# A decoder trunk on one core: the causal mask in VectorE's maximum, the forget gates' sums at the first HGRN2 step, the opening's norm in other tiles

## The chip, the core and the metric

The kernel runs on one core of a Trainium2 chip. Its engines work side by side, each through its own queue in strict order: TensorE (PE in the profile; PEld are its weight loads), VectorE (DVE), ScalarE (ACT), GpSimd (POOL) and SyncE (SP), which mostly issues DMAs. Semaphores tie them together. The metric is the device time of one execution in microseconds (us); less is better. The number given for a kernel is the median of its runs; the profile is of one more execution.

## The reference

Two layers, each a half-step SwiGLU, a mixer of three kinds of heads, and another half-step SwiGLU, with an RMSNorm ahead of each; 512 tokens, width 1024, all in float32. What the change touches is the opening (the first RMSNorm), the forget gates' running sum, and the masked softmax of the attention:

```python
for l in range(DEPTH):                                            # 2
    x = x + 0.5 * swiglu(rms_norm(x, ffn1_norm[l]), ffn1_w_in[l], ffn1_w_out[l])
    h = rms_norm(x, mix_norm[l]) @ w_mix_in[l]
    ...
    y = concat([short_conv_mixer(...), hgrn2_mixer(...), fox_mixer(...)])
    x = x + y @ w_mix_out[l]
    x = x + 0.5 * swiglu(rms_norm(x, ffn2_norm[l]), ffn2_w_in[l], ffn2_w_out[l])

def fox_mixer(q, k, v, f_logit, f_bias, q_gain, k_gain):         # 8 heads of 64
    ...
    log_f = log_sigmoid(f_logit + f_bias)
    cum = cumsum(log_f, axis=1).transpose(0, 2, 1)
    def block(i):                                                # 128 queries
        s = einsum('bhqd,bhkd->bhqk', qb, kh) + (cb[..., :, None] - cum[..., None, :])
        s = where(qpos[:, None] >= kpos[None, :], s, MASK_VALUE)
        p = softmax(s, axis=-1)
        return einsum('bhqk,bhkd->bhqd', p, vh)
```

## The kernel before, in words

Activations lie with features on the 128 partitions and the 512 tokens along a row. A float32 operand is split into a high half (a cast to fp32r) and a low half, the rest; a product takes three matmuls, high by high, high by low and low by high (`mm3`, lines 318, 324, 325). Weights come from HBM in granules: SP issues the DMAs into a tile `st` (line 290, two buffers), ACT casts the high half into a tile `hl` (line 307, three buffers), VectorE subtracts for the low half (line 308), and PE multiplies. The big matrices of the SwiGLU go through a scheme of halved products that adds and subtracts quarters first (lines 759 to 907).

What runs first on each engine is set by a tile scheduler from the order of the source and from priorities. Buffers come from pools: a tile asked for by a tag gets the next buffer of that tag, and its first writer waits until the readers of the tile that had it are done. Where `follow` is called, the order on an engine is fixed by hand; the DMAs of the opening on SP are one such chain.

**The opening** (`cover`, `open_stream`) runs in the first layer's first SwiGLU. It loads x, transposes it, scales it, and multiplies it with the first weight columns (lines 1657, 1666, 1667, 1710) while the squares for the norm are summed (`sqa`). `parted_norm` (line 418) splits the sum of squares into two tiles `sh`, two matmuls with a matrix of 1/1024 give the mean on all partitions (line 430), and `end_norm` makes `inv` of it. `lower_bounds` (line 944) then loads a few logits of HGRN2 into a tile `lb` of tag g1 (line 956). The two `sh` tiles have the tag g1 as well, with two buffers. `cover` goes on with the next weight columns, whose granules come from line 290.

**The mixer.** Ahead of HGRN2 its projections are made; the last of them also gives the attention's forget logits `zf`. `hgrn` is a generator of steps: after each the program takes a number of steps from `projections()`, the attention's q, k and v products, which keep PE busy. Its steps use the PSUM banks `pt` for transposes (line 1253) and for the output (`T`, line 1409). After it, `fox_decay` (line 1425) takes zf through log-sigmoid (lines 1429 to 1436), forms the running sum with eight matmuls by an upper triangle `utri` (line 1440, in a `pt` bank), and scales it into `negc` on ACT (line 1445) and VectorE (line 1446). `fox_prep` transposes q and k for each head (line 1495) and takes negc in as extra rows of the products.

**The attention** (`fox_attend`) runs in two halves of four heads. An item is a head and one of four query blocks i, over (i + 1) × 128 keys. `scores` puts two matmuls (lines 1521, 1522) and a third, the mask (line 1523: the identity by a tile of −1e30 above the diagonal, bf16), into a bank of PSUM; VectorE takes the negated maximum (line 1526); ACT takes the exponential with it as bias and sums the row (line 1528, printed as L270 since a helper issues it; from PSUM into a tile P of three buffers); VectorE inverts the sum (line 1529) and scales P (line 1533; ACT for i = 3). The scores run three items ahead (LOOK = 3). Item n is then transposed (line 1584), split (lines 1586, 1587) and multiplied with V (line 1543). Between them the program places the short convolution's and the output projection's matmuls as filler, each with its weight granules.

## Time and profile before

| what | us |
| --- | --- |
| runs | 1835.08, 1830.63, 1832.18 |
| median | 1832.18 |
| profiled execution | 1827.76 |
| its span, first to last instruction | 1826.0 |
| granted TensorE clock over it | 0.998 of full speed |

In a timeline row the first figure is the start in us from the span's beginning, the second the duration of what the row holds, then the engine, the line and the operation, output and inputs, their shape, and how many instructions were put together. In square brackets stands how long the engine had been idle before it and the instruction that ended the wait. In a row of a group (`x64: 230/231/236`) the durations are in ns: least, median, most. In a row of windows each engine's busy time follows its stretch and length, in the order PE, PEld, DVE, ACT, POOL, then the clock and the DMA engines' share. The two layers' attention runs from 484 to 588 and from 1383 to 1487 us.

### The profile page before, as it was taken

To read this page: it belongs to the slowest core of one execution; us is meant where nothing else is said; L and a number is where in the kernel's file an instruction comes from. 1 tells how busy PE (TensorE), PEld (TensorE's weight loads), DVE (VectorE), ACT (ScalarE), POOL (GpSimd) and SP (SyncE) were. 2 spreads that over 40 slices of the span, in tenths; PEclk is the share of its full clock that TensorE was granted. 3 is DMA by queue.
4 is the path that set the end of the run, shared out by engine and by line. 5 is a ranking of instruction groups with operands and counts; after the bars stand their busy time and mean duration, and the time that the engine had idled before them with its cause. 6 is when DMAs were issued, how large, how long until landed. Compare 5 with 4: busy or idle time off the path is not lost.

```text
span 1826.0 us, 34831 instructions
## 1 busy us (share of the span) xinstructions
PE 1809.0 (99%) x14345; PEld 1684.3 (92%) x14345; DVE 1466.3 (80%) x2017; ACT 989.9 (54%) x1402; POOL 169.5 (9%) x168
## 2 busy tenths in 40 slices
PE   8999999999999999999999999999999999999999
PEld 6899999899878899999889999998997788999997
DVE  8788888676797988879678887866858878888883
ACT  5455555454675565555445555555547665555551
POOL 0011020100000001112001111201000000020210
PEclk9999999999999999999999999999999999999999
DMA  5849684233322767868265787813333228677762
GB/s 147 233 109 199 171 174 113 70 88 83 87 71 92 216 141 163 191 168 174 81 193 137 162 191 194 165 64 82 83 82 82 76 93 231 162 152 195 153 137 92
DMA packets 243935, 250.94 MB, mean 137 GB/s; under 512 B 18457, under 2 KB 229153, under 8 KB 243777
## 3 DMA queue, kind: packets, MB, share of 16 engines
q1 hardware_dynamic: 189872, 182.38, 32.8%
q0 software_dynamic: 53600, 66.09, 22.7%
q8 instruction: 112, 1.84, 0.4%
q14 instruction: 47, 0.38, 0.1%
q10 hardware_dynamic: 304, 0.27, 0.0%
HBM read 223.98 MB, written 2.10 MB: 124 GB/s over the span
## 4 chain that ended last, share of the span: by engine, by line
PE 92%; DVE 3%; ACT 3%; DMA 1%; issue 1%; SPq 0%; ACTq 0%; DVEq 0%
PE mm L318 13%; PE mm L325 13%; PE mm L324 13%; PE sc L325 6%; PE sc L324 6%; PE sc L318 6%; PE pt L318 6%; PE pt L324 6%; PE pt L325 6%; PE po L318 3%; PE po L324 3%; PE po L325 3%; PE po L1543 1%; PE sc L1710 1%; PE pt L1710 1%
## 5 line engine op out<-in xcount | busy, mean ns | idle before, releaser
L786 ACT CAST hl<-w 128x1024 fp32r<-128x1024 f32 x322 | 337.5, 1051 | 317.9 <-PE mm L325 76.8
L788 DVE TENSOR_TENSOR hl<-w,hl 128x1024 fp32r<-128x1024 f32 x322 | 392.7, 1222 | 85.8 <-ACT hl L786 85.6
L307 ACT CAST hl<-st 128x512 fp32r<-128x512 f32 (+2 forms) x188 | 142.2, 756 | 190.3 <-PE po L325 67.8
L308 DVE TENSOR_TENSOR hl<-st,hl 128x512 fp32r<-128x512 f32 (+2 forms) x188 | 161.6, 860 | 100.3 <-ACT hl L307 98.6
L318 PE MATMUL mm<-xc,hl 128*128 128x256 f32 (+1 forms) x732 | 201.7, 276 | 0.5 <-ACT g L897 0.5
L325 PE MATMUL mm<-xc,hl 128*128 128x256 f32 x728 | 201.6, 277 | 0.0
L324 PE MATMUL mm<-xc,hl 128*128 128x256 f32 x728 | 201.5, 277 | 0.0
L325 PE MATMUL sc<-xc,hl 128*128 128x256 f32 x528 | 146.0, 277 | 0.0
L318 PE MATMUL sc<-xc,hl 128*128 128x256 f32 (+1 forms) x530 | 146.0, 276 | 0.0
L324 PE MATMUL sc<-xc,hl 128*128 128x256 f32 x528 | 145.9, 276 | 0.0
L318 PEld LDWEIGHTS mm<-xc,hl 128*128 128x128 f32 x732 | 137.3, 188 | 0.8 <-ACT g L897 0.7
L324 PEld LDWEIGHTS mm<-xc,hl 128*128 128x128 f32 x728 | 137.0, 188 | 0.0
L325 PEld LDWEIGHTS mm<-xc,hl 128*128 128x128 f32 x728 | 136.7, 188 | 0.1
L318 PE MATMUL pt<-xc,hl 128*128 128x256 f32 (+1 forms) x484 | 132.9, 276 | 0.0
L324 PE MATMUL pt<-xc,hl 128*128 128x256 f32 x480 | 132.7, 277 | 0.0
L325 PE MATMUL pt<-xc,hl 128*128 128x256 f32 x480 | 132.5, 276 | 0.0
L318 PE MATMUL mm<-x,hl 128*128 128x512 f32 x272 | 108.5, 399 | 6.0 <-ACT hl L307 5.6
L324 PE MATMUL mm<-x,hl 128*128 128x512 f32 x272 | 107.5, 395 | 0.0
L325 PE MATMUL mm<-x,hl 128*128 128x512 f32 x272 | 107.1, 394 | 0.0
L318 PEld LDWEIGHTS sc<-xc,hl 128*128 128x128 f32 x530 | 99.5, 188 | 0.2
L325 PEld LDWEIGHTS sc<-xc,hl 128*128 128x128 f32 x528 | 99.1, 188 | 0.1
L324 PEld LDWEIGHTS sc<-xc,hl 128*128 128x128 f32 x528 | 99.1, 188 | 0.0
(510 smaller groups left out, 5618.2 us busy)
## 6 DMA issues: line engine op xcount, KB each, us to landing
w<-in_ffn_w_in_dram SPq DMA_DIRECT2D x140, 512.0 KB, 5.2
w<-in_ffn_w_out_dram SPq DMA_DIRECT2D x64, 512.0 KB, 4.5
w<-in_ffn_w_out_dram POOLq DMA_DIRECT2D x56, 512.0 KB, 8.6
st<-in_w_mix_in_dram SPq DMA_DIRECT2D x88, 256.0 KB, 2.7
st<-in_ffn_w_in_dram SPq DMA_DIRECT2D x70, 256.0 KB, 3.3
w<-in_ffn_w_in_dram POOLq DMA_DIRECT2D x35, 512.0 KB, 8.5
w<-S POOLq DMA_DIRECT2D x35, 512.0 KB, 4.8
st<-in_ffn_w_out_dram SPq DMA_DIRECT2D x24, 512.0 KB, 4.6
```

Of the source, the lines that this page charges most:

```text
L307: a = nc.scalar.copy(hi, src[:, c : c + w])
L308: b = nc.vector.tensor_sub(lo, src[:, c : c + w], hi)
L318: i = nc.tensor.matmul(acc[:, c], ah, bh[:, c], start=first and c.start == 0, stop=False, skip_group_check=True,)
L324: nc.tensor.matmul(acc, ah, bl, start=False, stop=False, skip_group_check=True)
L325: i = nc.tensor.matmul(acc, al, bh, start=False, stop=last, skip_group_check=True)
L786: A(nc.scalar.copy(hi, src))
L788: return lambda: V(nc.vector.tensor_sub(lo, src, hi))
L1543: nc.tensor.matmul(self.ob[:, t0 + u * P : t0 + 2 * P], V[:, j, h % 4].rearrange("p a d -> p (a d)"), part[:, j, u:, :].rearrange("p i t - ...
L1710: E(nc.tensor.matmul(acc, wh[j][l][:, cols], (self.xh, self.xl)[r][k + j], start=k + j == 0 and which == 0, stop=k + j == KD - 1 and which ...
```

## The change

Three places change, and the tile `identb` (the identity in bf16) goes with the mask's matmul. In the opening the two `sh` tiles get the tags r0 and r1; the later callers keep theirs. `fox_decay` is called when the first step of `hgrn` has been issued. In the attention the third matmul goes; an instruction of VectorE adds a mask tile to the scores, negates the sum, writes it to P and takes the minimum, which is the bias as before; the exponential reads P in place with the scale −1. The mask tile (`zmask`, bf16, 384 zeros and the 128 of `maskb`) is made on GpSimd in each layer.

```diff
-        self.identb = c.tile([P, P], BF16, tag="identb", name="identb")
-        nc.vector.tensor_copy(self.identb, self.ident)
...
-    def parted_norm(self, pool, tag, bufs, keep=False):
-        nc = self.nc
-        hi, lo = (pool.tile([P, T], F32R, tag=tag, name=self.n("sh"), bufs=bufs) for _ in range(2))
+    def parted_norm(self, pool, tags, bufs, keep=False):
+        nc = self.nc
+        hi, lo = (pool.tile([P, T], F32R, tag=tag, name=self.n("sh"), bufs=bufs) for tag in tags)
...
             def norm():
                 self.end_norm(
                     self.bank("pt" if self.ntog % 2 == 0 else "po"), fp,
-                    self.parted_norm(fp, "g1", 2),
+                    self.parted_norm(fp, ("r0", "r1"), 1),
                 )
...
                 dense = projections()
-                for n in self.hgrn(l, hp, z, q, v, sg, og):
+                for part, n in enumerate(self.hgrn(l, hp, z, q, v, sg, og)):
+                    if part == 0:
+                        self.fox_decay(mp, zf)
                     for _ in range(n):
                         next(dense, None)
-                self.fox_decay(mp, zf)
...
+                self.zmask = ap_.tile([P, T], BF16, tag="zm", name=self.n("zm"))
+                nc.gpsimd.memset(self.zmask[:, : T - P], 0.0)
+                nc.gpsimd.tensor_copy(self.zmask[:, T - P :], self.maskb)
...
-            nc.tensor.matmul(sb[:, :n], QB[:, c], KB[:, :n], start=False, stop=False)
-            nc.tensor.matmul(sb[:, c], self.identb, self.maskb, start=False, stop=True)
+            nc.tensor.matmul(sb[:, :n], QB[:, c], KB[:, :n], start=False, stop=True)
             s1 = lambda tag: pool.tile([P, 1], F32, tag=tag, name=self.n(tag), bufs=3)
             nm, rs = s1("nm"), s1("rs")
-            nc.vector.tensor_reduce(nm, sb[:, :n], axis=AX.X, op=ALU.max, negate=True)
             pb = tl("P", 3)
-            self.act(pb[:, :n], sb[:, :n], AF.Exp, bias=nm, accum_out=rs)
+            nc.vector.tensor_tensor_reduce(
+                pb[:, :n], sb[:, :n], self.zmask[:, T - n :], -1.0, 3e38, ALU.add, ALU.min, nm
+            )
+            self.act(pb[:, :n], pb[:, :n], AF.Exp, bias=nm, scale=-1.0, accum_out=rs)
```

The lines move by a few: 290, 307, 318, 421, 430, 956 of before are 288, 305, 316, 419, 428, 954 now, 1253 and 1440 are 1255 and 1442, and 1526, 1529, 1533, 1584 are 1528, 1532, 1536, 1587.

In the opening, on SP, the last DMAs of `open_stream` (st_296), then `lb` and the next granules, with what each waits for; before:

```order
L1657 DMA st_296<-in_ffn_w_in_dram 128x2x256 [waits DMAHW2_49,DVE_49]
L1657 DMA st_296<-in_ffn_w_in_dram 128x2x256 [waits DMAHW3_49]
L956 DMA lb_457<-in_hgrn_lb_logits_dram 128x4x1 [waits DMAHW4_49,DVE_49,PE_49]
L290 DMA st_504<-in_ffn_w_in_dram 128x2x256 [waits DMAHW7_49,DMAHW6_49,DMAHW5_49]
L290 DMA st_504<-in_ffn_w_in_dram 128x2x256
```

and now:

```order
L1660 DMA st_296<-in_ffn_w_in_dram 128x2x256 [waits DMAHW2_49,DVE_49]
L1660 DMA st_296<-in_ffn_w_in_dram 128x2x256 [waits DMAHW3_49]
L954 DMA lb_455<-in_hgrn_lb_logits_dram 128x4x1 [waits DMAHW4_49]
L288 DMA st_502<-in_ffn_w_in_dram 128x2x256 [waits DMAHW6_49,DMAHW7_49,DMAHW5_49,DVE_49]
L288 DMA st_502<-in_ffn_w_in_dram 128x2x256
```

`lb` no longer waits for PE or VectorE, and the first granule waits for VectorE itself. On ACT, in the same place, the cast of this granule (hl_507, now hl_505) stood behind `sh` and the norm's activations:

```order
L1666 COPY hl_299<-st_296 128x512
L391 ACTIVATE x_48_305<-po_271,gain_88 128x512
L1666 COPY hl_299<-st_296 128x512
L407 ACTIVATE sq_323<-mm_266 128x512
L407 ACTIVATE sq_327<-po_271 128x512
L421 COPY sh_411<-sqa_158 128x512
L270 ACTIVATE nr_417<-po_410,epsc 128x512
L270 ACTIVATE nr_417<-nr_417 128x512
L270 ACTIVATE nt_418<-nr_417 128x512
L307 COPY hl_507<-st_504 128x1024
```

and now:

```order
L1669 COPY hl_299<-st_296 128x512
L305 COPY hl_505<-st_502 128x1024
L389 ACTIVATE x_48_305<-po_271,gain_88 128x512
L1669 COPY hl_299<-st_296 128x512
L405 ACTIVATE sq_323<-mm_266 128x512
L405 ACTIVATE sq_327<-po_271 128x512
L268 ACTIVATE lb_455<-lb_455 128x4
L305 COPY hl_535<-st_532 128x1024
L419 COPY sh_409<-sqa_158 128x512
L305 COPY hl_565<-st_562 128x1024
L268 ACTIVATE nr_415<-po_408,epsc 128x512
```

It stands between the two casts of the opening's last granule, and the next granule's cast ahead of `sh`.

At the first step of HGRN2, on PE, projections (mm), the transposes of HGRN2's `T` and the eight matmuls of the running sum; before:

```order
L318 MATMUL mm_4141<-hl_4144,x_381_3575 128x256
L324 MATMUL mm_4141<-hl_4144,x_381_3575 128x256
L325 MATMUL mm_4141<-hl_4144,x_381_3575 128x256
L1253 MATMUL pt_4175<-ident,T_4171 128x128 x4
L1253 MATMUL pt_4181<-ident,T_4171 128x128 x4
L318 MATMUL mm_4140<-hl_4195,x_383_3582 128x256
```

and now:

```order
L316 MATMUL mm_4161<-hl_4164,x_381_3573 128x256
L322 MATMUL mm_4161<-hl_4164,x_381_3573 128x256
L1442 MATMUL pt_4147<-utri,flh_4143 8x512
L1442 MATMUL pt_4147<-utri,fll_4144 8x512
L1442 MATMUL pt_4147<-utri,flh_4143 8x384
L1442 MATMUL pt_4147<-utri,fll_4144 8x384
...
L1442 MATMUL pt_4147<-utri,fll_4144 8x128
L323 MATMUL mm_4161<-hl_4164,x_381_3573 128x256
L1255 MATMUL pt_4195<-ident,T_4191 128x128 x4
```

The sum stands ahead of the last of 24 projection matmuls and of the transposes.

At the start of the attention's first half, on VectorE, the first items' maximum, inverse and scaling; before:

```order
L1526 TENSOR_REDUCE nm_5445<-sc_5441 128x1 [waits PE_49]
L1526 TENSOR_REDUCE nm_5456<-sc_5452 128x1 [waits PE_49]
L1529 RECIPROCAL rs_5446<-rs_5446 128x1 [waits Activation_49]
L1533 TENSOR_SCALAR P_5448<-P_5448,rs_5446 128x128 [waits DVE_49]
L1529 RECIPROCAL rs_5457<-rs_5457 128x1 [waits Activation_49]
```

and now:

```order
L1528 ISA P_5447,nm_5445<-sc_5442,zm_5418 128x128 [waits PE_49]
L1528 ISA nm_5445 128x1
L1528 ISA P_5457,nm_5455<-sc_5452,zm_5418 128x256 [waits PE_49]
L1528 ISA nm_5455 128x1
L1528 ISA P_5467,nm_5465<-sc_5462,zm_5418 128x384 [waits PE_49]
L1528 ISA nm_5465 128x1
L1532 RECIPROCAL rs_5446<-rs_5446 128x1 [waits Activation_49]
```

Each maximum is now two instructions, the first of which writes a tile P and reads the mask tile zm.

More of the change, by code (lines that the diff above doesn't have):

```diff
@@ L577, in enter @@
             next(first)
-        parts = self.parted_norm(fp, "g1", 2, True)
+        parts = self.parted_norm(fp, ("g1", "g1"), 2, True)
         nb = self.bank("pt" if self.ntog % 2 == 0 else "po")
@@ L1053, in mix @@
                 norm = lambda: self.end_norm(
-                    self.bank("pt"), hp, self.parted_norm(hp, self.tt, self.tb)
+                    self.bank("pt"), hp, self.parted_norm(hp, (self.tt,) * 2, self.tb)
                 )
```

## The prediction

> **What bounds the kernel now.** I read the page's busy times and its chain of waits first, because a removed instruction is worth its time only on the engine that the chain follows.

> ```profile
> PE 1809.0 (99%) x14345; PEld 1684.3 (92%) x14345; DVE 1466.3 (80%) x2017; ACT 989.9 (54%) x1402; POOL 169.5 (9%) x168
> ...
> PE 92%; DVE 3%; ACT 3%; DMA 1%; issue 1%; SPq 0%; ACTq 0%; DVEq 0%
> ```

> The end is set by TensorE (PE). Work taken from VectorE (DVE) or ScalarE (ACT) is worth nothing unless PE waits for it, and the three parts of the change are to be priced as PE time: a stall that goes, a stall that comes, an instruction that goes. The sum is made against the profiled execution, 1827.76 us with a span of 1826.0; the runs' median, 1832.18, is 4.4 above it and all three runs lie above it, so I apply the difference to the median. About 0.3%, 5.5 us, is the least that a measurement of this kernel can tell from no change.

> Then I read the timeline at the three places. The opening first:

> ```profile
> 14.96 0.88 SPq L1657 DMA_DIRECT2D st<-in_ffn_w_in_dram  x2
> ...
> 31.87 0.63 PE L430 MATMUL po<-sh,ones_mean 128*128 128x512 f32 x2
> 32.30 0.37 SPq L956 DMA_DIRECT2D lb<-in_hgrn_lb_logits_dram  x1
> 32.78 9.16 SPq L290 DMA_DIRECT2D st<-in_ffn_w_in_dram  x8
> ...
> 36.98 1.05 ACT L307 CAST hl<-st 128x1024 fp32r<-128x1024 f32 x1 [2.38 <-DMA st<-in_ffn_w_in_dram]
> ...
> 38.08 0.80 PE L318 MATMUL mm<-x,hl 128*128 128x512 f32 x1 [5.58 <-ACT hl L307]
> ...
> 41.54 0.40 PE L325 MATMUL mm<-x,hl 128*128 128x512 f32 x1
> ...
> 41.77 0.40 PE L318 MATMUL po<-x,hl 128*128 128x512 f32 x1
> ```

> This is the longest stall of the program. SP issues nothing from 15.84 to 32.30 us: its next DMA loads `lb` into a buffer of the pool tag g1, whose last readers are the norm's two matmuls (L430), and the eight weight loads of L290 stand behind it. PE waits 5.58 us for the first of them. It then runs cold: eight matmuls take 38.08 to 41.54, 3.46 us, where eight at the later pitch of 41.77 − 41.54 = 0.23 take 1.84, so 1.62 us more are lost.

> [...]

> **Part 1, the opening.** sh's halves go to the tags r0 and r1, so `lb` waits for no norm, and the loads can issue as soon as their own buffers are free. The first needs the slot that the last cover weights but one leave; VectorE finishes with that slot at 20.66:

> ```profile
> 19.99 0.67 DVE L1667 TENSOR_TENSOR hl<-st,hl 128x512 fp32r<-128x512 f32 x1
> ```

> From issue to the cast took 36.98 − 32.78 = 4.2 us, so the first weights are there by 20.66 + 4.2 = 24.9, before the cover's last matmuls end, and PE gets its next work without a gap. It is not free. The granule's cast (1.05 on ACT) and subtraction (1.22 on VectorE, by the row of its shape below) now stand ahead of the last cover weights, and the second granule's ahead of sh, so the norm's matmuls come some 4 us later; followed by hand through the three queues, each push-back leaves PE a small wait, 0.35, 0.2 and 0.75, 1.3 us in all, an estimate. Gain at the spot: 5.58 + 1.62 − 1.3 = 5.9 us. Does it last? The next place where PE needs something made by VectorE after the norm is the first product on `xc`:

> ```profile
> 76.74 1.22 DVE L788 TENSOR_TENSOR hl<-w,hl 128x1024 fp32r<-128x1024 f32 x1
> ...
> 83.28 0.33 PE L318 MATMUL mm<-xc,hl 128*128 128x128 f32 x2
> ```

> It is ready at 77.96 and needed at 83.28, a cover of 5.3 us; PE being 5.9 earlier wants it at 77.4. VectorE's own start there depends on a norm that comes later, though it has by then done three granules' subtractions, 3.7 us, in advance. I let 0.7 us of the gain be lost there and take **−5.2**. Bounds: −7.2 (no new wait) and −2.5 (VectorE two or three more us late at 77).

> **Part 2, fox_decay at the first HGRN step.** The small operations already ran early; the eight cumulative matmuls (L1440) ran at the end of HGRN2.

> ```profile
> 393.26 0.19 DVE L1429 SCALAR_TENSOR_TENSOR fa<-zf 128x32 f32<-128x32 f32 x1
> ...
> 393.50 0.28 PE L325 MATMUL mm<-hl,x 128*128 128x256 f32 x1
> 393.61 1.04 PE L1253 MATMUL pt<-ident,T 128*128 128x128 f32 x8
> ...
> 394.24 0.22 ACT L1435 CAST flh<-fl 128x32 fp32r<-128x32 f32 x1 [0.26 <-DVE fl L1432]
> ...
> 394.50 0.19 DVE L1436 TENSOR_TENSOR fll<-fl,flh 128x32 fp32r<-128x32 f32 x1 [0.28 <-ACT flh L1435]
> ...
> 473.33 0.40 PE L1440 MATMUL pt<-utri,flh 128*8 128x512 f32 x1 [0.78 <-DVE T L1409]
> ...
> 474.53 0.66 PE L1495 MATMUL pt<-ident,qk 128*128 128x128 f32 x4
> ...
> 476.91 0.67 DVE L1446 SCALAR_TENSOR_TENSOR negc<-pt,negc 8x512 fp32r<-8x512 f32 x1
> ...
> 487.86 0.50 PE L318 MATMUL mm<-x,hl 128*128 128x512 f32 x1 [0.23 <-ACT cy L1181]
> ```

> Their 474.53 − 473.33 = 1.2 us is moved, not removed. In the new order they stand behind 23 of the 24 projections that end here, so PE reaches them at 393.50; `flh` is ready at 394.46, `fll` at 394.69. PE then waits 1.0 us in order, with the 24th projection and the transposes behind, where the trace shows no wait. At the old place the 0.78 us wait for VectorE's T does not go: the transposes of L1495 use the same bank and inherit it. What does go there is the scaling, 0.67 us of VectorE (L1446) and as much of ACT, ahead of the output of HGRN2 that PE waits for at 487.86; I give it 0.4. Net +0.6 a layer, **+1.2** for two. Bounds: −1.5 (the boundary's waits go too) and +3 (both waits stay and VectorE passes on the delay of its L1446, which now waits in its queue at 394).

> **Part 3, the mask.** 64 matmuls and weight loads leave PE. By busy time that is 14.8 us, but matmuls overlap, so what counts is the distance between the starts of their neighbours.

> ```profile
> L1523 PE MATMUL sc<-maskb,identb x64: 230/231/236, 489.1 to 1474.4; 128*128 128x128 bf16 x64
> ```
> ```profile
> 489.06 0.23 PE L1523 MATMUL sc<-maskb,identb 128*128 128x128 bf16 x1
> 489.10 0.36 PE L1521 MATMUL sc<-KA,QA 128*128 128x256 f32 x1
> ...
> 489.43 0.23 PE L1523 MATMUL sc<-maskb,identb 128*128 128x128 bf16 x1
> 489.46 0.48 PE L324 MATMUL mm<-x,hl 128*128 128x512 f32 x1
> ...
> 489.78 0.39 PE L325 MATMUL mm<-x,hl 128*128 128x512 f32 x1
> ```

> The next matmul starts 0.03 to 0.04 us after a mask. A wide one right behind it holds PE 489.78 − 489.46 = 0.32 us, not the warm pitch of 0.23, so such a mask costs 0.04 + 0.09 = 0.13; one before a score costs nearer 0.05. I take 0.092: 64 × 0.092 = −5.9 us. Ends: 64 × 0.04 = −2.6 and −14.8.

> VectorE pays for it. The maximum, TENSOR_REDUCE, becomes an instruction with two inputs and a full output, followed by one that reads the accumulator; neither is in the trace. The nearest rows:

> ```profile
> 491.65 0.69 DVE L1526 TENSOR_REDUCE nm<-sc 128x1 f32<-128x512 f32 x1
> ```
> ```profile
> L906 DVE TENSOR_TENSOR g<-g,mm x13: 679/687/689, 102.0 to 1201.0; 128x512 f32<-128x512 f32 x13
> ...
> L1235 DVE TENSOR_TENSOR_SCAN b<-smask,lf x4: 1202/1210/1217, 381.4 to 1281.4; 128x512 f32<-128x512 f32 x4
> ...
> L1529 DVE RECIPROCAL rs<-rs x64: 143/163/166, 490.1 to 1476.4; 128x1 f32<-128x1 f32 x64
> ```

> [...] The read costs at most a RECIPROCAL of one column, 0.163. I take the addition's rate, since the operands are its operands, and 0.12 for the read: 32 × 0.12 = 3.8 us of VectorE a layer. Where does that show?

> ```profile
> 484.00:500.00 16.00, 15.77 (x91) 12.30 (x90) 13.15 (x34) 12.41 (x30) 1.52 (x3) 1.00 0.40 100
> 500.00:520.00 20.00, 19.36 (x111) 15.12 (x110) 19.68 (x46) 14.96 (x37) 0.52 (x1) 1.00 0.27 70
> 520.00:540.00 20.00, 19.64 (x111) 14.87 (x109) 18.05 (x39) 14.45 (x33) 1.07 (x2) 1.00 0.27 78
> ...
> 560.00:588.00 28.00, 27.77 (x149) 22.26 (x148) 19.46 (x38) 15.49 (x31) 0.00 (x0) 1.00 0.36 114
> ```

> The third figure is VectorE: full at 19.68 of 20 in the second window, 8.5 us free in the last. In the first four heads each 0.12 us lands on an engine that has nothing free and that also makes the low halves (L308) on which PE's filler matmuls wait. So of 2.95 us a layer taken from PE I let 1.75 be given back: −1.2 a layer, **−2.4** in all. Exp now reads SBUF instead of PSUM; the nearest pair is

> ```profile
> L1531 ACT ACTIVATE P<-P,rs x16: 719/724/727, 493.7 to 1476.7; 128x512 f32<-128x512 f32 x16
> ...
> 492.65 0.70 ACT L270 ACTIVATE P<-sc,nm 128x512 f32<-128x512 f32 x1
> ```

> 0.02 us more each, 64 × 0.02 = 1.3 us if it weren't hidden by ACT's idle quarter (14.96 of 20 busy). POOL's fill of the mask tile is hidden by an engine 9% busy, before the first scores. Bounds of part 3: −6, and +5 if the first half is VectorE's.

> Sum: −5.2 + 1.2 − 2.4 = **−6.4 us**, 1821.4 on the profiled execution, **1825.8** against the median.

> **The rivals.** *VectorE becomes the bound: slower.* Exp now works in place in a P tile that the new instruction writes, and there are three. So the instruction for item n+3 waits on the transposes of item n, in VectorE's strict order, with the low halves queued behind it, and PE waits for those. Against it:

> ```profile
> 491.97 0.38 PE L1584 MATMUL pt<-ident,P 128*128 128x128 f32 x2
> ...
> 492.83 0.23 PE L1523 MATMUL sc<-maskb,identb 128*128 128x128 bf16 x1
> ```

> item 1's transposes end at 492.35, before item 4's scores are complete, so the slot is mostly free in time. For it: the full window above. The 32 items of the two layers' first halves, at 0.3 us held up and 0.45 more body and read (the scan's surplus of 0.52 at 512 columns, 0.33 as the mean of the four widths, and 0.12), add 32 × 0.75 = 24 us against 2.85 + 0.32 + 1.5 = 4.6 us free in each half (the windows from 484 to 535); 14.8 us remain, less 2.95 for the masks of the other halves, and with the opening and the decay 14.8 − 2.95 − 5.2 + 1.2 = +7.8: **1840**. It decides from 0.3 us an item more (4.6/16). [...] 17%.

> *The moves don't move: no change.* The waits reappear: the fox wait at 1.0 a layer stays unpaid (+2), the opening gives −3, attention's gain is eaten by VectorE: −1 to −3, **1830**. For it: PE's waits at 473 and 487 are short, and the work that follows inherits them. 20%.

> *The mask is worth more.* Without its weight load PE saves 0.13 in every place and VectorE's surplus hides: −5.9 − 6 + 0.5 = −11.4, **1820.8**. For it: PE is 96.8% busy even in the full window, so VectorE was not stopping it much. 18%.

> **How the numbers follow.** My forecast has 45%, with a range of its own from 1823 to 1829. Faster than 1826.7 is two thirds of it and all of the last rival; slower than 1837.7 nearly all of the first; the rest is within 0.3%: 0.49, 0.34, 0.17. The range, 1819 to 1837, takes in the second and the last rival and the edge of the first.

> **What would show it.** Step 1: SP issuing weights near 21 us, no PE stall over 1 us before 40, and no cold pitch at 38; a wait of PE before 80 for `hl` or `xc` would show the loss. Step 2: PE waiting about 1 us at 393 for `flh` and still 0.8 at 473. Step 3: the new instruction at 0.69 us for 512 columns and its read at 0.06 to 0.16; more than that, with PE waiting for L308's product between 490 and 535, makes the prediction wrong, as does a norm so late that VectorE holds PE at 77.

## The result, and the profile after

The changed kernel takes 1824.09 us (median of 6 runs, 1821.32 to 1826.67) beside 1831.39 of the kernel before (6 runs, 1829.33 to 1835.08): a ratio of 0.9958, with a 95% interval from 0.9943 to 0.9973. That is 7.3 us by the medians and 4.9 to 10.4 by the interval. The forecast was 6.4 less.

The page of the profiled execution, busy times and chain:

```profile
PE 1808.0 (99%) x14281; PEld 1686.0 (92%) x14281; DVE 1467.5 (80%) x2080; ACT 989.6 (54%) x1402; POOL 170.4 (9%) x172
```

64 instructions fewer on PE, and its busy time is only 1 us less: busy time did not tell what the change was worth. The timeline does. The opening of the changed kernel:

```profile
15.86 0.47 SPq L954 DMA_DIRECT2D lb<-in_hgrn_lb_logits_dram  x1
...
20.71 14.48 SPq L288 DMA_DIRECT2D st<-in_ffn_w_in_dram  x8
...
24.36 1.05 ACT L305 CAST hl<-st 128x1024 fp32r<-128x1024 f32 x1
...
26.98 0.39 PE L316 MATMUL mm<-x,hl 128*128 128x512 f32 x1
27.21 0.39 PE L322 MATMUL mm<-x,hl 128*128 128x512 f32 x1
27.96 0.50 PE L323 MATMUL mm<-x,hl 128*128 128x512 f32 x1 [0.36 <-DVE hl L306]
...
34.94 0.50 PE L428 MATMUL po<-sh,ones_mean 128*128 128x512 f32 x1 [0.57 <-DVE sh L419]
```

The load of `lb` issues at 15.86 instead of 32.30, the weights at 20.71 instead of 32.78, and PE's first product on them starts at 26.98 instead of 38.08, between the matmuls of the cover. The wait of 5.58 us is gone; 0.36 and 0.57 stand in its place. The windows from 30 to 50 us, of before and then of the changed kernel, show the clock as well (the figure behind POOL's busy time):

```profile
30.00:50.00 20.00, 14.42 (x57) 11.28 (x57) 16.16 (x33) 9.80 (x12) 1.44 (x1) 0.83 0.65 194
```
```profile
30.00:50.00 20.00, 19.43 (x86) 15.68 (x85) 19.11 (x50) 12.12 (x15) 1.44 (x1) 1.00 0.91 252
```

86 matmuls where there were 57, and a granted clock of 1.00 instead of 0.83: the cold stretch went with the wait.

At the first step of HGRN2 and at its end the changed kernel shows:

```profile
388.21 0.22 ACT L1437 CAST flh<-fl 128x32 fp32r<-128x32 f32 x1 [0.26 <-DVE fl L1434]
...
388.48 0.39 PE L1442 MATMUL pt<-utri,flh 128*8 128x512 f32 x1 [0.86 <-ACT flh L1437]
...
469.36 0.66 PE L1497 MATMUL pt<-ident,qk 128*128 128x128 f32 x4 [0.95 <-DVE T L1411]
```

The new wait for `flh` is 0.86 us, and the old one for VectorE's T is still there, 0.95, now ahead of the transposes.

The group of VectorE's new instruction, with the durations' least, median and most in ns, and what it waited for:

```profile
L1528 DVE CUSTOM_DVE_ANT_0 P<-sc,zm x64: 270/476/693, 485.3 to 1471.7; 128x128 f32<-128x128 f32 x16, 128x256 f32<-128x256 f32 x16, 128x384 f32<-128x384 f32 x16, 128x512 f32<-128x512 f32 x16
L1528 DVE DVE_READ_ACCUMULATOR2_ANT nm<- x64: 71/83/91, 485.5 to 1472.4; 128x1 f32 x64
...
its engine sat idle before it (us, times) until:
  PE pt L1587: 6.2, 10
  PE sc L1524: 1.7, 3
```

It takes what the reduction took (270, 476 and 693 ns, beside 271, 478 and 693 of L1526 before), the read takes 0.083 us, and VectorE waited 6.2 us for P tiles to come free. With the scores in PSUM and the mask tile in bf16 as sources, 512 columns take 0.693 us at most, beside 0.687 of the addition of L906 before.

Both kernels run the same products, most of them in the same order, so the same matmul can be found in both timelines, and the differences of the starts give what each stage took. At the product that stands at 100.2 us before, the changed kernel is 5.99 us ahead; its HGRN2 stages are 0.75 and 0.27 us longer in the two layers, and its attentions 0.73 and 0.64 shorter.

The spans of the two profiled executions, 1826.0 and 1823.6, differ by only 2.4, because this execution of the changed kernel lost some 4 us in a stage that the change doesn't touch; that is shown in the last section.

### The profile page after: what moved, and what is told of

It is laid out like the page before. It is cut to its first block, busy times and chain, and to the rows that moved or that the text cites. A ratio compares the mean times of both kernels' runs of the same rounds, so it can differ in the third digit from the quotient of the medians.

```text
span 1823.6 us, 34797 instructions
## 1 busy us (share of the span) xinstructions
PE 1808.0 (99%) x14281; PEld 1686.0 (92%) x14281; DVE 1467.5 (80%) x2080; ACT 989.6 (54%) x1402; POOL 170.4 (9%) x172
## 3 DMA queue, kind: packets, MB, share of 16 engines
q8 instruction: 112, 1.84, 0.4%
## 4 chain that ended last, share of the span: by engine, by line
PE 90%; DVE 5%; ACT 3%; issue 1%; DMA 1%; SPq 0%; ACTq 0%; DVEq 0%
PE mm L316 13%; PE mm L323 13%; PE mm L322 13%; PE sc L323 6%; PE sc L322 6%; PE sc L316 6%; PE pt L316 6%; PE pt L322 6%; PE pt L323 6%; PE po L316 3%; PE po L322 3%; PE po L323 3%; DVE hl L306 1%; PE po L1546 1%; PE pt L1587 1%
```

## The experiments

The table has every run's ratio to the kernel before on the same chip, and three readings of its profiled execution by the starts of the same products: the lead over the kernel before at the product that stands there at 100.2 us, the length of HGRN2 with the projections (from the product at 391.1 of before to that at 485.2, and 1291.2 to 1384.2 in the second layer), and of the attention (485.2 to 590.1, and 1384.2 to 1490.6). e1 to e4 ran on one chip, e5 to e8 on a second, e9 to e12 on a third, where the kernel before took 1835.8 us instead of 1831 to 1832; so ratios are best compared within such a group.

| kernel | ratio, 95% interval | lead at 100 | HGRN2, layers 1, 2 | attention, layers 1, 2 |
| --- | --- | --- | --- | --- |
| before | | 0 | 94.10, 93.04 | 104.89, 106.35 |
| changed | 0.9958 [0.9943, 0.9973] | 5.99 | 94.85, 93.31 | 104.16, 105.71 |
| e1_opening | 0.9969 [0.9955, 0.9983] | 6.15 | 93.83, 92.55 | 106.45, 105.62 |
| e2_sums | 1.0011 [0.9996, 1.0025] | -0.60 | 94.75, 93.39 | 105.35, 105.54 |
| e3_mask | 0.9994 [0.9976, 1.0012] | -0.76 | 94.71, 92.32 | 104.06, 104.73 |
| e4_no_sums | 0.9950 [0.9935, 0.9965] | 6.29 | 94.12, 92.54 | 104.42, 105.09 |
| e5_sums_later | 0.9950 [0.9935, 0.9964] | 6.05 | 94.23, 92.87 | 104.33, 105.14 |
| e6_psum | 0.9966 [0.9951, 0.9980] | 6.23 | 94.74, 93.33 | 103.94, 104.59 |
| e7_no_mask | 0.9967 [0.9955, 0.9980] | -1.42 | 94.08, 92.73 | 103.24, 104.43 |
| e8_lb_gpsimd | 1.0001 [0.9984, 1.0019] | -0.67 | 94.85, 92.54 | 106.61, 105.60 |
| e9_lb_tile | 0.9939 [0.9916, 0.9962] | 5.82 | 94.02, 92.51 | 104.93, 105.66 |
| e10_dve_short | 0.9954 [0.9924, 0.9984] | 5.55 | 94.47, 93.36 | 104.41, 106.31 |
| e11_dve_long | 1.0085 [1.0061, 1.0108] | 6.38 | 94.50, 93.38 | 116.64, 118.16 |
| e12_no_sums_psum | 0.9936 [0.9916, 0.9957] | 4.88 | 93.85, 92.56 | 103.43, 104.65 |

**Each part alone, and the change without its second part.** e1 is the kernel before with the tags of the opening, e2 with the earlier call of `fox_decay`, e3 with the attention's lines of the change, e4 the changed kernel with the call put back where it was:

```diff
 # e1_opening, to before
-  self.parted_norm(fp, "g1", 2),
+  self.parted_norm(fp, ("r0", "r1"), 1),
 # e2_sums, to before
-  for n in self.hgrn(l, hp, z, q, v, sg, og):
+  for part, n in enumerate(self.hgrn(l, hp, z, q, v, sg, og)):
+      if part == 0:
+          self.fox_decay(mp, zf)
       for _ in range(n):
           next(dense, None)
-  self.fox_decay(mp, zf)
```

> The kernel before with the opening's part alone. If the stall behind the load of lb was the whole of it: the first product on the next granule starts 11.1 us earlier than before, as in the changed kernel, PE is 6.0 us ahead at 100 us, and stays 6.0 ahead to the end: 1825.4 beside 1831.4. If VectorE, whose norm comes later, passes the lateness on: less than 4 us ahead at 100 us, 1828 or more.

Measured: 0.9969, 5.7 us less with an interval of 3.1 to 8.2, and a lead of 6.15 us at 100 us. The lead is made in the opening alone and by the runs' times nothing later takes it back; the first theory holds. (In this execution the first attention, which e1 doesn't change, was 1.6 us longer than before's, of which 1.0 is a wait of PE for the DMA of a tile KA; that is how far one execution's stages go apart.)

> The kernel before with the forget gates' sums at the first HGRN2 step alone. If the move only exchanges one wait for another: about 0.9 us of a new wait for flh at that step, 1.2 us of matmuls that come back at the end of HGRN2, where the transposes of q and k take over the old wait: +0.4 to +0.8 us a layer, 1832.6. If leaving the end of HGRN2 shorter pays: the old wait of 0.8 goes, -0.5 us a layer, 1830.4.

Measured: 1.0011, +2.0 us with an interval of −0.7 to +4.6. HGRN2 is 0.65 and 0.35 us longer than before's, and PE waits for flh here too:

```profile
396.09 0.39 PE L1441 MATMUL pt<-utri,flh 128*8 128x512 f32 x1 [0.87 <-ACT flh L1436]
```

The time alone leaves it open; by the stages, of this run and of the others below, the move costs and does not pay.

> The kernel before with the mask's part alone (and its identity tile gone). If the mask's matmul costs PE 0.09 us and VectorE gives half of it back: -0.6 to -1.2 us a layer, 1829.5. If the mask costs what its busy time says: -14.8 us, 1816.6. If VectorE's queue, held up at the P tiles, is the bound: slower, +3 us or more.

Measured: 0.9994, −1.1 us with an interval of −4.4 to +2.2. The time cannot tell it from nothing, but it rules out −14.8 and a loss of 3. The attention's stages are 0.83 and 1.62 us shorter than before's.

> The changed kernel with the sums put back to the end of HGRN2. If they cost as the two profiles show (0.8 us in the first layer, 0.4 in the second): 1.2 us below the changed kernel, 1822.9. If the move pays by way of the attention's start: above it, 1825 or more.

Measured: 0.9950, beside 0.9958 of the whole change. The two intervals overlap; HGRN2's stages are 0.73 and 0.77 shorter than the changed kernel's, 1.5 us, near what was expected.

**What in the opening does it.** e8 leaves the tiles as they were and moves only the load to another queue, out of the chain that `follow` fixes; e9 leaves the norm's tiles and gives `lb` one of its own:

```diff
 # e8_lb_gpsimd
-  self.follow("s", nc.sync.dma_start(lg, logits.rearrange("l (r p) -> p l r", p=P)))
+  nc.gpsimd.dma_start(lg, logits.rearrange("l (r p) -> p l r", p=P))
 # e9_lb_tile
-  self.lower_bounds(logits, fp.tile([P, T], F32, tag="g1", name=self.n("lb"), bufs=2))
+  self.lower_bounds(logits, fp.tile([P, T], F32, tag="r0", name=self.n("lb"), bufs=1))
```

> The kernel before, but the load of the logits lb is issued by GpSimd's queue instead of SyncE's; sh keeps its tag g1, so lb still waits for the norm. If the cause of the 5.58 us stall is that the granules stand behind that waiting load in SP's queue: the granules issue at 21 us as in the changed kernel, PE is 6 us ahead of before at 100 us, 1825.3. If the tag itself matters (the place of sh, not the queue): PE gains less than 3 us, 1829 or more.

Measured: 1.0001 [0.9984, 1.0019], no gain at all, which the first theory did not foresee. Its timeline says why:

```profile
20.69 14.23 SPq L290 DMA_DIRECT2D st<-in_ffn_w_in_dram  x8
...
34.66 0.50 PE L430 MATMUL po<-sh,ones_mean 128*128 128x512 f32 x1
...
35.28 0.92 POOL L956 DMA_DIRECT2D lb<-in_hgrn_lb_logits_dram  x1 [33.62 <-PE po L430]
...
42.20 0.29 DVE L958 COPY lb<-lb 128x2 f32<-128x2 f32 x1 [5.94 <-DMA lb<-in_hgrn_lb_logits_dram]
42.28 0.68 DVE L414 SCALAR_TENSOR_TENSOR nt<-po,nt 128x512 f32<-128x512 f32 x1
...
43.02 0.77 PE L318 MATMUL po<-x,hl 128*128 128x512 f32 x1 [4.89 <-DVE nt L414]
```

The weights issue at 20.69, as expected: SP's queue was what held them. But `lb` still waits for the norm, and its first reader on VectorE (L958) stands ahead of the norm's own L414. VectorE waits 5.94 us for the load, L414 comes late, and PE waits 4.89 us for the bank that L414 reads. In the kernel before VectorE did not wait there:

```profile
34.64 0.69 DVE L414 SCALAR_TENSOR_TENSOR nt<-po,nt 128x512 f32<-128x512 f32 x1 [3.08 <-ACT nt L270]
35.25 0.16 DVE L958 COPY lb<-lb 128x2 f32<-128x2 f32 x1
```

There L414 stands first, and the load that SP issued at 32.30 is in by 35.25; GpSimd issues it at 35.28, and the reader that waits for it starts at 42.20, 6.9 us after the issue. So e8 frees SP's queue and, with a slower load and another order on VectorE, makes a new stall of about the old one's size. It doesn't price the queue; e1 and e9 do.

> The kernel before with one tag changed: lb gets a tile of its own (r0), the norm's sh keeps g1. If the whole gain of the opening comes from a load of lb that waits for nothing, it appears here too: PE 6.0 to 6.3 us ahead of before at 100 us, 1825. If moving sh is needed, less than 3.

Measured: 0.9939 [0.9916, 0.9962], a lead of 5.82 us. Freeing the load from the norm is all that the opening's gain needs; moving sh was one way to do it.

**The place of the sums.** e5 calls `fox_decay` one step later (`if part == 1`), where the transposes of that step stand ahead of the eight matmuls.

> The changed kernel with the sums one HGRN2 step later, behind that step's transposes. If what the move costs is PE's wait of 0.86 us for flh: the wait goes in both layers, and PE stands 0.7 us nearer to its lead of 6.0 at 398 (-4.8 rather than -3.7 beside before, of which 1.2 come back at the end of HGRN2), 1822.5. If the matmuls' own place costs: no difference, 1824.

Measured: 0.9950, and the wait for flh is gone, but the next one shows at once:

```profile
388.54 1.03 PE L1255 MATMUL pt<-ident,T 128*128 128x128 f32 x8
...
390.38 0.40 PE L1442 MATMUL pt<-utri,flh 128*8 128x512 f32 x1 [0.45 <-ACT T L1258]
```

PE waits 0.45 us for the `pt` bank that ACT still empties. HGRN2 is 0.62 and 0.44 shorter than in the changed kernel, 1.1 of the 1.4 expected. So the lateness of flh was most of the price; the wait for the bank is the likely rest.

**The mask's price on PE.** e7 takes the third matmul out of the kernel before and changes nothing else, so its diagonal blocks go unmasked.

```diff
-  nc.tensor.matmul(sb[:, :n], QB[:, c], KB[:, :n], start=False, stop=False)
-  nc.tensor.matmul(sb[:, c], self.identb, self.maskb, start=False, stop=True)
+  nc.tensor.matmul(sb[:, :n], QB[:, c], KB[:, :n], start=False, stop=True)
```

> The kernel before with the mask's matmul left out and nothing in its place: the keys of a diagonal block are not masked, VectorE's and ACT's instructions are as before. It prices the matmul alone. If it costs PE 0.09 us and VectorE does not stop PE: -2.9 us a layer in the attention, 1825.4. If VectorE gives nothing back in the changed kernel, the matmul is worth what the mask's part showed, 0.7 to 1.2 us a layer, 1829. By busy time: -7.4 a layer, 1816.5.

Measured: 0.9967, −6.0 us with an interval of −3.7 to −8.2. The two attention stages sum to 207.67. Five executions with the mask on PE (before, e1, e2, e8, e9) sum to 210.59 to 212.21, mean 211.40, so by this one execution the matmul is worth 3.7 us, 0.058 each. That is the low end of what the runs say, and their 6.0 is the forecast's 5.9. The starts in the trace show the price at single places, here at the place that the prediction read, of before and then of e7:

```profile
489.30 0.28 PE L1522 MATMUL sc<-KB,QB 66*128 66x256 f32 x1
...
489.78 0.39 PE L325 MATMUL mm<-x,hl 128*128 128x512 f32 x1
```
```profile
490.63 0.28 PE L1522 MATMUL sc<-KB,QB 66*128 66x256 f32 x1
490.75 0.39 PE L324 MATMUL mm<-x,hl 128*128 128x512 f32 x1
490.98 0.39 PE L325 MATMUL mm<-x,hl 128*128 128x512 f32 x1
```

From L1522 to L325 it takes 0.35 us, and with the mask it took 0.48, so such a mask costs 0.13, as reckoned. Where transposes follow it costs 0.07. At the 30 of the 64 places where at least the next two matmuls are the same in both kernels the median is 0.076, which would be 4.9 us for all. The matmul is thus worth 4 to 6 us, a quarter to two fifths of its 14.8 busy; the runs don't tell closer.

**VectorE's share.** e6 writes the sum in place into PSUM, so that no P tile is waited for; e10 and e11 add a reduction of 128 or 512 columns per item, whose result nothing reads:

```diff
 # e6_psum, to the changed kernel
-  pb[:, :n], sb[:, :n], self.zmask[:, T - n :], -1.0, 3e38, ALU.add, ALU.min, nm
+  sb[:, :n], sb[:, :n], self.zmask[:, T - n :], -1.0, 3e38, ALU.add, ALU.min, nm
...
-  self.act(pb[:, :n], pb[:, :n], AF.Exp, bias=nm, scale=-1.0, accum_out=rs)
+  self.act(pb[:, :n], sb[:, :n], AF.Exp, bias=nm, scale=-1.0, accum_out=rs)
 # e10_dve_short (e11_dve_long: [:, :512])
+  nc.vector.tensor_reduce(s1("dm"), self.smask[:, :128], axis=AX.X, op=ALU.max)
```

> The changed kernel, but VectorE's new instruction writes its sum back into the scores' bank and the exponential reads that bank, so it no longer waits for a P tile to come free (6.2 us of VectorE's waits for transposes in the two layers). If VectorE has the time for these waits: the attention's length stays within 0.5 us a layer, 1824. If the waits held PE up: 1 us a layer less or more, 1822 or below. A bank that is held longer could cost as much: 1826.

Measured: 0.9966 [0.9951, 0.9980]; the attentions sum to 208.53, beside 208.79 to 209.87 (mean 209.41) of the four executions with the new instruction as it is (changed, e3, e4, e5). It is 0.9 us shorter, less than these differ among themselves (1.1), but e12 below has the same edit and 208.1, and both lie under all four. What these two lack shows at the start of each attention of the changed kernel:

```profile
486.27 0.56 DVE L1528 CUSTOM_DVE_ANT_0 P<-sc,zm 128x384 f32<-128x384 f32 x1 [0.36 <-PE sc L1524]
...
486.95 0.84 DVE L1536 TENSOR_SCALAR P<-P,rs 128x128 f32<-128x128 f32 x2
...
487.80 0.30 PE L1587 MATMUL pt<-ident,P 128*128 128x128 f32 x1 [0.56 <-DVE P L1536]
```

VectorE takes the third item's maximum, for which it waits, ahead of the first items' scaling, and PE waits 0.56 us for that, 1.1 in the two layers. e3, e4 and e5 have this wait too, the kernel before and e6 don't, and e12 has 0.2 of it a layer. So of the 1 us the order of VectorE's instructions is the likelier source, and the waits for P tiles as such cost little or nothing.

> The changed kernel with one more reduction of 128 columns on VectorE for each item, 0.27 us, whose result nothing reads. VectorE's free time in the attention's first half was put at 4.6 us in 16 items, 0.29 each, so it should just hold: the two attentions 0 to 2 us longer together, 1825. If VectorE is the bound already: 16 x 0.27 = 4.3 a layer, 1833.

Measured: the added reduction takes 0.276 us (median), and the attentions sum to 210.72, 1.3 more than the mean of 209.41. The first attention is 0.2 longer than the mean of the four, the second 1.1, and there the clock fell (last section). So VectorE holds, and more easily than expected: 17.7 us more of its time cost PE hardly anything.

> The same with a reduction of 512 columns, 0.69 us an item. By the prediction's rival VectorE then binds in the first half of each attention: 16 x 0.69 - 4.6 = 6.4 us a layer, 12.9 in all, 1837. If the queues absorb it: under 4 us.

Measured: 1.0085, and the attentions are 12.5 us longer each than the changed kernel's, 24.9 in all, twice the 12.9 expected. The windows of the first attention:

```profile
494.00:514.00 20.00, 19.65 (x106) 15.24 (x104) 19.38 (x49) 14.15 (x31) 0.66 (x2) 1.00 0.30 80
514.00:534.00 20.00, 16.44 (x85) 12.66 (x84) 19.41 (x48) 13.00 (x28) 0.52 (x1) 0.91 0.12 36
534.00:554.00 20.00, 14.88 (x78) 11.12 (x77) 19.32 (x52) 11.84 (x30) 1.04 (x2) 0.95 0.26 71
554.00:582.00 28.00, 27.98 (x137) 23.39 (x137) 25.06 (x62) 16.91 (x37) 0.00 (x0) 0.91 0.31 93
```

VectorE is at 19.3 to 19.4 of 20 in three windows and PE down to 14.88: this is what a bound on VectorE looks like, and the changed kernel is not there. The clock fell as well, to 0.91, 0.95 and 0.91 in the last three, which is 5.3 us of full clock and so at most that much of the 12.5. By the starts of the scores, 6.0 of the 12.5 are lost by the middle of the attention and the rest behind it.

**The two improvements together.** e12 is e4 with e6's edit.

> The changed kernel with the sums back at the end of HGRN2 and VectorE's sum written in place into the scores' bank. By the profiles so far the first is worth 1.2 us and the second 0.9, if they add: 1822 beside 1824.1. If the longer held bank takes the second back: 1823.

Measured: 0.9936 [0.9916, 0.9957], the best ratio, but e9, which has the opening's gain alone, has 0.9939 on the same chip, and the interval overlaps that of the whole change as well: the times do not show that the two add. By stages it is 1.75 us shorter than the changed kernel in HGRN2 and 1.8 in the attentions; part of that lies within the spread of single executions.

## Why the prediction was right, and where its terms were off

The time alone, 4.9 to 10.4 less, doesn't tell the forecast's 6.4 from the measured 7.3; what bears the three terms out is the stages and the runs of single parts.

**Part 1, −5.2; measured −6.0** beside the profiled execution of before, and 6.6 between the means of e1, e4, e5, e6, e9, e10, e11, e12 and the changed kernel (5.93) and of before, e2, e3, e7 (−0.70). The mechanism was right: `lb` behind the norm in SP's queue, then 5.58 us idle and 1.62 cold. That the small waits would bring no cold stretch of their own, and the 1.62 come back whole, was an estimate; the granted clock of 1.00 from 30 to 50 us agrees with it. The new small waits, put at 1.3, are 0.93. The mis-sized steps are the small waits and the 0.7 us that was to be lost at the first product on `xc` because VectorE would come later there:

```profile
73.80 2.35 DVE L786 TENSOR_TENSOR hl<-w,hl 128x1024 fp32r<-128x1024 f32 x2
...
77.25 0.33 PE L316 MATMUL mm<-xc,hl 128*128 128x128 f32 x2
```

VectorE starts on it at 73.80, 2.9 us earlier than before's 76.74, and the product follows at 77.25 with no wait. The norm did come later (its step on VectorE, L414 before, at 37.59 instead of 34.64), but SP issued the weights of this stage earlier too (line 757 now, at 59.61 instead of 64.44), and VectorE still had them ready in time, with a cover of about 1 us.

**Part 2, +1.2; measured +1.2.** HGRN2's stages sum to 188.02 in the mean where the sums stand at its first step (changed, e2, e6, e10, e11) and to 186.79 where they stand at its end (before, e1, e3, e4, e7, e8, e9, e12). The new wait was put at 1.0 and is 0.86; the old one, forecast to be inherited by the transposes, was inherited, 0.95 beside 0.78. The 0.4 that was to come back from VectorE's shorter end has no row of its own. The stages fit it: in the first layer 0.86 and 0.17 more of waiting made the stage only 0.75 longer.

**Part 3, −2.4; measured −2.0** (209.41 beside 211.40, where single executions of either kind go 1.1 to 1.6 apart). By the runs of e3 it is −1.1, between −4.4 and +2.2. The net was right within that. Its terms are known less well: the matmul, put at 5.9, is 3.7 by e7's stages, 4.9 by its single places and 6.0 by its runs, and what comes back, put at 3.5, is 1.7 by the stages. The accumulator's read was put at 0.12 and is 0.083, and the body at the addition's rate, as measured (0.693 beside 0.687 for 512 columns). What the traces don't bear out is why something comes back. The prediction had it from a VectorE with no time left; e10 adds three times as much VectorE time as the reads do and costs hardly anything, and 1.1 of the 1.7 are the two waits of PE behind VectorE's new order at the start of the attentions. That the net agreed is in part luck.

**The sum.** −6.6, +1.2 and −2.0 make −7.4; the medians say −7.3; at that closeness, beside an interval 5.5 us wide, it is no more than agreement.

**The rivals.** The one that ends slower needed 0.3 us an item more on VectorE. The scan's surplus that it reckoned with, 1.21 − 0.69 = 0.52, did not come: the new instruction takes 0.693. e10, with 0.276, costs 1.3 us; e11, with 0.68, costs 24.9: the point lies between them, which agrees with where it was put. Past it the price is twice what e11 was expected to cost by that rival: that let only the first half of each attention be bound, where the second half lost as much, and had no fall of the clock in it. The head-of-line wait on P tiles is real (6.2 us of VectorE's time) and lands on free time. That the moves only move their waits held for the sums and not for the opening. That the mask would be worth more, 11.4 us in all with 0.13 in every place, fell with the interval of the whole change, which ends at 10.4, and with the 0.07 where transposes follow.

## What to carry to other kernels

A DMA that waits for a buffer held everything behind it in its queue here (SP issued nothing from 15.84 to 32.30 us), and in e8 the first reader of what it loads held the queue of the engine that reads, for 5.94 us; look for a small load with a late buffer ahead of large ones, and free the load itself before moving it to another queue. A short matmul among pipelined ones costs PE the distance that it puts between its neighbours' starts, 0.07 to 0.13 us of its 0.23 at the places read here. Work added to an engine can cost by the order that it brings more than by its time (1.1 of the 1.7 us that came back here): look at the first items of a loop. When a small stage is moved earlier, its inputs' readiness at the new place must be read first: 0.2 us operations in a row on two engines made flh 0.9 us late.

## What was not expected of the hardware

**The clock fell without a long wait.** In e10 PE waited 1.12 and then 0.36 us within some 3 us:

```profile
1432.80 0.30 PE L1523 MATMUL sc<-KA,QA 128*128 128x128 f32 x1 [1.12 <-DVE dm L1531]
...
1434.34 0.50 PE L322 MATMUL mm<-fyl,hl 128*128 128x512 f32 x1 [0.36 <-DVE fyl L1565]
```
```profile
1434.00:1435.00 1.00, 0.66 (x2) 0.59 (x3) 0.97 (x6) 0.47 (x3) 0.00 (x0) 0.85 0.19 45
1435.00:1436.00 1.00, 1.00 (x4) 0.93 (x3) 0.90 (x4) 0.51 (x3) 0.00 (x0) 0.50 0.00 0
1436.00:1437.00 1.00, 1.00 (x4) 0.71 (x4) 1.00 (x5) 0.00 (x0) 0.12 (x1) 0.50 0.00 0
1437.00:1438.00 1.00, 1.00 (x4) 0.81 (x3) 0.17 (x1) 0.35 (x1) 0.44 (x1) 0.50 0.00 0
1438.00:1439.00 1.00, 1.00 (x9) 0.92 (x8) 0.70 (x3) 0.98 (x4) 0.00 (x0) 0.94 0.01 4
```

**The same matmuls ran slower for 110 us, at full clock.** From 1000 to 1110 us both kernels are in the first product stage of a SwiGLU, with PE busy all the time and nothing changed. Before, then the changed kernel:

```profile
1000.00:1110.00 110.00, 110.00 (x972) 110.00 (x971) 93.65 (x98) 60.40 (x69) 16.59 (x14) 1.00 0.77 177
```
```profile
1000.00:1110.00 110.00, 110.00 (x936) 110.00 (x935) 89.11 (x91) 57.57 (x65) 14.40 (x12) 1.00 0.75 175
```

36 matmuls fewer in the same time, 0.1175 us each instead of 0.1132, 4% slower, or 4.1 us: that is why the profiled spans differ by less than the medians. e10 and e12 have the same stretch at the same place, e12 a second one from 1578 to 1677 and e5 one from 674 to 773; the other executions have only 14 to 28 us of it at a time. What brings it about was not found.
